# A hybrid encoder layer on one core: the gate of block 1 ahead of block 0's last denominators, one residual and its store near the end

## The chip, the cores and the metric

The kernel runs on one core of one Trainium2 chip. The metric is the time of one execution in device microseconds (us); lower is better. Five engines work side by side, each through its own queue in program order: TensorE (PE, matmuls), VectorE (DVE), ScalarE (ACT), GpSimd (POOL), and SyncE (SP), which issues all DMAs of this kernel. Engines wait for each other through semaphores.

## What is computed

The layer takes x (4096 tokens of 1024 numbers, float32), normalises it, projects it once to queries, keys, values, two gates and a pooling input, runs windowed attention and multi-scale pooling side by side, and adds the normalised output projection to x:

```
h = rmsnorm(x, pre_norm_g)
q, k, v, g_a, u_p, g_p = split(h @ w_in)
a = banded_attention(q, k, v, rel_bias, attn_sink) * silu(g_a)   # |i-j| <= 128
p = multiscale_pool(u_p, pool_w, pool_scale) * silu(g_p)
mixed = concat([a, p]) @ w_out
x = x + rmsnorm(mixed, post_norm_g)
```

There are 8 query heads of 64 and 2 key/value heads. Attention works in blocks of 128 queries, each against its own block of keys and the two beside it, with a sink logit in the denominator.

## The kernel before, in words

Matrix products run in float16, every float32 operand being split into a high and a low half and three of the four products of halves summed in PSUM.

The first half of the program forms the gates g_a and g_p and the pooling, and leaves their results in DRAM. The second half, which the change touches, goes through the tokens from the end to the start in units of 256 tokens (u = 15 down to 0), each of two blocks of 128 (block b = 2u and 2u + 1). Per unit it projects keys, values and queries, and then for each block:

- `scores(b, half)`: PE writes the logits of four heads (a half) to the PSUM tiles `s0` and `s1`.
- `logits(b, half, i)`: DVE adds the bias to a head's logits and finds the row extremum, from PSUM into the SBUF tile `p` (line 1295, a main instruction and a short one that reads `nm`). The first of the four issues a small POOL copy.
- `exps`: ACT takes the exponential and the row sum (line 1306); `denominators`: DVE scales the sums and takes reciprocals (lines 1313 and 1316).
- `probs` and `rests`: ACT writes the high half of the normalised probabilities (line 1328), DVE the low half (line 1336), both in `pn`; `turn`: a transposing DMA on SP puts them into `pt` (line 1345).
- `values(b, bank)`: PE multiplies `pt` with the values into two PSUM tiles, `o` and one named `p` in the bank `acc0`, `acc1` or `acc2` that the call names (line 1438; for block 0 the second tile is `s1`).
- `gate(b)`: DVE multiplies both tiles with the gate g_a into `at` (line 1462, two instructions). With that the two PSUM tiles are free.

The output projection of a unit is made from seven products in a Strassen-like scheme (`product`, line 1588, of inputs "11", "12", "22" and the sums "s1" to "s4"), and for unit 0 from eight plain ones (`last_product`, line 1560; its accumulators are named `z`, one of them lying in `s0`). `high` (ACT, line 1490) and `low` (POOL or DVE, line 1494) split an input of a product; `add` (DVE, line 1627) sums products into the output tile, `gain` (line 1622) multiplies it with post_norm_g, `square` (ACT) and `mean` (DVE line 1640 and POOL line 1645) give the factor `rs`, `residual(u, i, ...)` (DVE, line 1649) scales it and adds x, and `store` (SP, line 1655) writes it out. The residual of unit u with i = 1 is that of block 2u.

The accumulator of `last_product(1, "22", O22, 1, True)`, the first product for the right 512 columns of block 0, lies in `acc2`. The last earlier user of `acc2` is `values(1, 2)`. So this product can start only when `gate(1)` has read that tile. Likewise `last_product(0, "12", O21, 0, True)` writes `acc1` and needs the `add` that reads unit 1's product "s4" out of it.

The order of every engine's work is written out by hand: each step is entered with a number (`due(t, ...)`, or `at_(t, ...)` relative to the start `z` of the last stretch), all steps are sorted by that number, and each engine's instructions are issued in that order. The number is no time; it only sets the order. `ending(u, i, tm, tr)` enters a `mean` at `tm`, a `residual` at `tr` and its `store` at `tr + 1.3`. The change is in the last stretch, which holds the last part of unit 2, and units 1 and 0.

Of the kernel before, what the change touches and what calls it, by code (L numbers as in the profile page):

```python
# [134 lines left out]
def hybrid_layer(ctx: ExitStack, tc, io, out):  # L135
# [1107 lines left out]
    def due(t, fn, *args):  # L1243
        plan.append((t, len(plan), fn, args))
# [505 lines left out]
    def at_(t, fn, *args):  # L1750
        due(z + t, fn, *args)
# [11 lines left out]
    def cast(th, tw, u, name, f, eng):  # L1763
        at_(th, high, u, name, f)
        at_(tw, low, u, name, f, eng)

    def ending(u, i, tm, tr, split=False):
        at_(tm, mean, u, i)
        for n, cs in enumerate((LO, HI) if split else (slice(0, D),)):
            at_(tr + 0.7 * n, residual, u, i, cs)  # L1770
            at_(tr + 1.3 + 0.7 * n, store, u, i, cs)
# [187 lines left out]
    at_(12.3, square, 2, 0, 1)  # L1959
    at_(11.1, gain, 2, 1, LO, V)  # L1960
    at_(11.8, gain, 2, 1, HI, V)
    ending(2, 1, 10.9, 23.0)
    at_(38.7, gain, 2, 0, HI, V)
    ending(2, 0, 13.8, 39.4)

# [27 lines left out]

    cast(24.7, 26.1, 0, "22", a22, G)
    cast(34.35, 35.0, 0, "12", a12, G)
    at_(37.0, gate, 1)
    cast(37.6, 38.6, 0, "11", a11, V)
    at_(45.9, gate, 0)
    cast(46.7, 47.3, 0, "21", a21, V)
# [95 lines left out]
```

## Time and profile before

| what | value |
|---|---|
| median of 3 runs | 1182.24 us (1181.93 to 1183.64) |
| the profiled execution, whole | 1181.88 us |
| its span in the profile | 1179.9 us |
| PE busy | 1150.8 us, 98% of the span, 14304 matmuls |
| DVE busy | 932.0 us, 79% |
| ACT busy | 702.7 us, 60% |
| POOL busy | 310.2 us, 26% |

The span runs from the first to the last recorded instruction; the whole execution is 1.98 us longer. Times in the trace count from the start of the span. In the timeline, columns are start, duration, engine, line, operation, output and inputs, shape and count; brackets at the end give the idle time of the engine before the row and what ended it. Matmuls are pipelined, so a row's end overlaps the next row's start a little.

### The profile page before, as it was taken

To read this page: it belongs to the slowest core of one execution; us is meant where nothing else is said; L and a number is where in the kernel's file an instruction comes from. 1 tells how busy PE (TensorE), PEld (TensorE's weight loads), DVE (VectorE), ACT (ScalarE), POOL (GpSimd) and SP (SyncE) were. 2 spreads that over 40 slices of the span, in tenths; PEclk is the share of its full clock that TensorE was granted. 3 is DMA by queue.
4 is the path that set the end of the run, shared out by engine and by line. 5 is a ranking of instruction groups with operands and counts; after the bars stand their busy time and mean duration, and the time that the engine had idled before them with its cause. 6 is when DMAs were issued, how large, how long until landed. Compare 5 with 4: busy or idle time off the path is not lost. (4 is left out here: it accounts for less than half of the span.)

```text
span 1179.9 us, 33946 instructions
## 1 busy us (share of the span) xinstructions
PE 1150.8 (98%) x14304; PEld 883.7 (75%) x14304; DVE 932.0 (79%) x1865; ACT 702.7 (60%) x1459; POOL 310.2 (26%) x310
## 2 busy tenths in 40 slices
PE   5999999999999999999999999999999999999987
PEld 4998888888888888986677576666767667666643
DVE  6889997858788983568877877887787797788785
ACT  5875655545655542257676566667667666666761
POOL 0002111101101110201534433533443353254231
PEclk9999999999999999999999999999999999999998
DMA  8644487577757574299985777786687678686783
GB/s 314 217 111 166 161 270 261 178 239 229 239 188 236 158 188 159 67 275 245 222 198 141 189 193 149 188 197 184 137 188 205 140 196 184 176 169 154 190 205 107
DMA packets 292441, 224.65 MB, mean 190 GB/s; under 512 B 210704, under 2 KB 251920, under 8 KB 287680
## 3 DMA queue, kind: packets, MB, share of 16 engines
q1 hardware_dynamic: 292288, 222.48, 69.5%
q8 instruction: 112, 1.84, 0.6%
q14 instruction: 41, 0.34, 0.1%
HBM read 113.37 MB, written 60.33 MB: 147 GB/s over the span
## 5 line engine op out<-in xcount | busy, mean ns | idle before, releaser
L634 PEld LDWEIGHTS <-wq 128*128 128x128 f16 x4104 | 401.4, 98 | 52.8 <-issue 2.8
L634 PE MATMUL y<-xt,wq 128*128 128x256 f16 x1512 | 204.1, 273 | 0.9 <-ACT cc L742 0.9
L1306 ACT ACTIVATE p<-p,nm 128x385 f32<-128x385 f32 (+1 forms) x256 | 152.8, 599 | 37.1 <-POOL p L1289 20.4
L1227 PE MATMUL aq<-xb,xb 128*128 128x256 f16 x1024 | 173.4, 273 | 0.1
L1588 PE MATMUL ms<-wo,ys 128*128 128x512 f16 x720 | 162.7, 379 | 0.3 <-DVE mo L1627 0.3
L1336 DVE SCALAR_TENSOR_TENSOR pn<-p,rd,pn 128x384 f16<-128x384 f32 (+1 forms) x256 | 156.0, 660 | 6.4 <-ACT pn L1328 6.4
L1295 DVE CUSTOM_DVE_ANT_0 p<-s,nt,nsink 128x384 f32<-128x384 f32 (+1 forms) x256 | 155.9, 665 | 1.8 <-PE s L1272 1.7
L1227 PEld LDWEIGHTS <-xb 128*128 128x128 f16 x1280 | 125.2, 98 | 22.6 <-issue 6.3
L1227 PE MATMUL aq<-xb,xt 128*128 128x256 f16 x512 | 139.6, 273 | 0.0
L1328 ACT ACTIVATE pn<-p,rd 128x384 f16<-128x384 f32 (+1 forms) x256 | 134.5, 596 | 4.2 <-issue 1.1
L1588 PEld LDWEIGHTS <-ys 128*128 128x128 f16 x720 | 69.1, 98 | 81.6 <-issue 3.1
L304 POOL TENSOR_TENSOR yt<-yt,sg 128x512 f32<-128x512 f32 (+2 forms) x32 | 47.9, 1498 | 311.4 <-DVE yt L307 307.2
L1588 PE MATMUL m<-wo,y 128*128 128x512 f16 x540 | 121.8, 379 | 0.0
L1588 PEld LDWEIGHTS <-y 128*128 128x128 f16 x540 | 51.4, 98 | 63.0 <-issue 2.9
L1622 POOL TENSOR_TENSOR mo<-mo,gpost 128x512 f32<-128x512 f32 x39 | 63.8, 1635 | 94.6 <-ACT jkb L1611 93.4
L634 PE MATMUL plain<-xb,wq 128*128 128x256 f16 x576 | 68.8, 276 | 3.0 <-ACT xb L446 1.8
L1227 PEld LDWEIGHTS <-xt 128*128 128x128 f16 x640 | 62.6, 98 | 8.3
L634 PE MATMUL y<-xb,wq 128*128 128x256 f16 x504 | 68.8, 273 | 0.0
L634 PE MATMUL v<-xb,wq 128*128 128x256 f16 x504 | 68.6, 273 | 0.2 <-DVE cc L304 0.2
L634 PE MATMUL v<-xt,wq 128*128 128x256 f16 x504 | 68.6, 273 | 0.0
L634 PE MATMUL x<-xb,wq 128*128 128x256 f16 x504 | 68.2, 273 | 0.0
L1272 PE MATMUL s<-k_all,q 64*32 64x288 f16 (+7 forms) x3648 | 62.7, 266 | 2.1 <-DVE nm L1295 1.2
(212 smaller groups left out, 1911.6 us busy)
## 6 DMA issues: line engine op xcount, KB each, us to landing
nt<-in_xT SPq DMA_DIRECT2D x28, 512.0 KB, 5.1
x_scr<-xb SPq DMA_DIRECT2D x14, 1024.0 KB, 7.2
xb<-x_scr SPq DMA_DIRECT2D x14, 1024.0 KB, 7.1
xr<-in_x SPq DMA_DIRECT2D x28, 512.0 KB, 4.6
out<-xr SPq DMA_DIRECT2D x28, 512.0 KB, 2.6
xn<-in_x SPq DMA_DIRECT2D x27, 512.0 KB, 4.4
ga_scr<-cc SPq DMA_DIRECT2D x64, 128.0 KB, 2.4
raw<-in_w_out SPq DMA_DIRECT2D x16, 512.0 KB, 5.4
```

Of the source, the lines that this page charges most:

```text
L304: eng.tensor_tensor(out=out, in0=in0, in1=in1, op=op)
L634: nc.tensor.matmul(b[:, s], wq[:, slot[q, op], wv, s, k, :], x[:, xv, k, :], start=(first and k + s + wv + xv == 0), stop=(last and k == H ...
L1227: nc.tensor.matmul(acc, w[:, j, k, :], x[:, kh, v, kt, :], start=(n == 0), stop=(n == 3 * KT - 1),)
L1272: nc.tensor.matmul(s_ps[qs, gg, c0:c1], q_t[u, half][a, qi, jj, tl + 32 * hq : tl + 32 * hq + 32], k_all[a, ki, kc + c0 - s0 : kc + c1 - s ...
L1295: nc.vector.tensor_tensor_reduce(out=p_t[b, half][:, hh, :nk], in0=s_t[jj][:, gg, :nk], in1=bias[:, h, lo : lo + nk], scale=negc[:, h : h ...
L1306: nc.scalar.activation(p[:, hh, : nk + 1], p[:, hh, : nk + 1], AF.Exp, bias=nm_t[b, half][:, hh : hh + 1], scale=-1.0, accum_out=den_t[b, ...
L1328: nc.scalar.activation(prob_view(b, half)[:, 0, i], p_t[b, half][:, i, :nk], AF.Copy, scale=rd_t[b, half][:, i : i + 1],)
L1336: nc.vector.scalar_tensor_tensor(out=pn4[:, 1, i], in0=p_t[b, half][:, i, :nk], scalar=rd_t[b, half][:, i : i + 1], in1=pn4[:, 0, i], op0= ...
L1588: nc.tensor.matmul(z_t[u, tag], y[:, k, yi, :], wo[o][:, wi, k, :], start=(n == 0 and acc is None), stop=(n == 3 * HK - 1), skip_group_che ...
L1622: eng.tensor_tensor(out=mo, in0=mo, in1=gpost[:, cs], op=ALU.mult)
```

## The change

Two numbers in the list are changed: the residual of unit 2 with i = 1 (and its store), and the gate of block 1.

```diff
-    ending(2, 1, 10.9, 23.0)
+    ending(2, 1, 10.9, 38.2)
...
-    at_(37.0, gate, 1)
+    at_(33.9, gate, 1)
     cast(37.6, 38.6, 0, "11", a11, V)
```

No instruction is added or removed. On VectorE, at the end of the softmax of block 1, there stands before: the last low halves of block 1 (`pn_1_18718`), the residual (`xr_18224`), and then the logits of block 0's first half.

```order
L1336 SCALAR_TENSOR_TENSOR pn_1_18718<-p_1_18616,rd_1_18615,pn_1_18718 128x384 x2
L1627 TENSOR_TENSOR xb_68<-ms_1_18705,xb_68 128x512
L1336 SCALAR_TENSOR_TENSOR pn_1_18718<-p_1_18616,rd_1_18615,pn_1_18718 128x384 x2
L1649 SCALAR_TENSOR_TENSOR xr_18224<-mo_1_17912,rs_1_18459,xr_18224 128x1024
L1295 ISA p_0_18751,nm_0_18748<-s_5946,nt,nsink,negc 128x256
L1295 ISA nm_0_18748 128x1
```

With the change the logits follow the low halves directly (buffer numbers shift by a few):

```order
L1336 SCALAR_TENSOR_TENSOR pn_1_18718<-p_1_18616,rd_1_18615,pn_1_18718 128x384 x2
L1627 TENSOR_TENSOR xb_68<-ms_1_18705,xb_68 128x512
L1336 SCALAR_TENSOR_TENSOR pn_1_18718<-p_1_18616,rd_1_18615,pn_1_18718 128x384 x2
L1295 ISA p_0_18749,nm_0_18746<-s_5946,nt,nsink,negc 128x256
L1295 ISA nm_0_18746 128x1
```

The residual has left this place; every DVE row after it stands one place earlier.

Further on, still on VectorE, after the last of the logits of block 0's second half, there stand before: the denominators (`den_1`, `rd_1`), the low halves (`pn_1`), the `add` of unit 1's product "s4", the two instructions of block 1's gate (`at`), and the low half of input "11" (`xt_67<-at`).

```order
L1295 ISA nm_1_18858 128x1
L1313 TENSOR_SCALAR den_1_18859<-den_1_18859 128x4
L1316 RECIPROCAL rd_1_18860<-den_1_18859 128x4
L1336 SCALAR_TENSOR_TENSOR pn_1_18962<-p_1_18861,rd_1_18860,pn_1_18962 128x256 x4
L1627 TENSOR_TENSOR xb_68<-ms_1_18757,xb_68 128x512
L1462 SCALAR_TENSOR_TENSOR at_18988<-o_18867,gaf,gb_18400 128x4x64
L1462 SCALAR_TENSOR_TENSOR at_18988<-p_18866,gaf,gb_18400 128x4x64
L1494 TENSOR_TENSOR xt_67<-at_18988,xt_67 128x4x128
```

With the change:

```order
L1295 ISA nm_1_18856 128x1
L1462 SCALAR_TENSOR_TENSOR at_18944<-o_18865,gaf,gb_18400 128x4x64
L1462 SCALAR_TENSOR_TENSOR at_18944<-p_18864,gaf,gb_18400 128x4x64
L1313 TENSOR_SCALAR den_1_18857<-den_1_18857 128x4
L1316 RECIPROCAL rd_1_18858<-den_1_18857 128x4
L1336 SCALAR_TENSOR_TENSOR pn_1_18963<-p_1_18859,rd_1_18858,pn_1_18963 128x256 x4
L1627 TENSOR_TENSOR xb_68<-ms_1_18755,xb_68 128x512
L1649 SCALAR_TENSOR_TENSOR xr_18224<-mo_1_17912,rs_1_18459,xr_18224 128x1024
L1494 TENSOR_TENSOR xt_67<-at_18944,xt_67 128x4x128
```

The gate has moved ahead of the denominators, past seven instructions, and the residual now stands behind the `add`, before the low half of "11".

On SP, the store of that residual (`out<-xr_18224`) moves from behind block 1's last transposing DMA (`pt_1`, 24 tiles) to behind both of block 0's (`pt_0` and `pt_1`, 16 tiles each); the load of the pooling input (`yf`) and both transposes move up by one.

```order
 L1658 DMA wo_5956<-w_scr 128x4096
-L1345 DMA_TRANSPOSE pt_1_18742<-pn_1_18718 128x24x128
+L1345 DMA_TRANSPOSE pt_1_18741<-pn_1_18718 128x24x128
+L1517 DMA yf_0_18774<-yp_scr 128x512
+L1345 DMA_TRANSPOSE pt_0_18862<-pn_0_18844 128x16x128
+L1345 DMA_TRANSPOSE pt_1_18973<-pn_1_18963 128x16x128
 L1655 DMA out<-xr_18224 128x1024
-L1517 DMA yf_0_18776<-yp_scr 128x512
-L1345 DMA_TRANSPOSE pt_0_18864<-pn_0_18846 128x16x128
-L1345 DMA_TRANSPOSE pt_1_18972<-pn_1_18962 128x16x128
 L1655 DMA out<-xr_18226 128x1024
```

PE, ACT and POOL have the same instructions in the same order as before.

## The prediction

> **What bounds the kernel now.** PE is busy for 98% of the span (table above), so I ask first where it still waits in the second half of the program. The view of waits, for PE alone from 850 us to the end, has two rows:
>
> ```profile
> PE z L1560 <- DVE at L1462: 4.0, 1, 4.0
> PE s L1272 <- DVE nm L1295: 1.2, 2, 0.8
> ```
>
> Both name DVE, and both are places of the change: line 1462 is the gate, line 1295 the logits. The timeline of PE shows where they lie (in brackets, the wait):
>
> ```profile
> 1130.46 7.94 PE L1588 MATMUL ms<-wo,ys 128*128 128x512 f16 x36
> 1139.18 0.52 PE L1272 MATMUL s<-k_all,q 64*32 64x160 f16 x24 [0.78 <-DVE nm L1295]
> 1140.11 0.52 PE L1272 MATMUL s<-k_all,q 64*32 64x160 f16 x24 [0.41 <-DVE nm L1295]
> 1140.71 2.75 PE L1560 MATMUL z<-wo,xt 128*128 128x512 f16 x12
> ...
> 1145.32 2.76 PE L1588 MATMUL ms<-wo,ys 128*128 128x512 f16 x12
> 1152.06 7.04 PE L1560 MATMUL z<-wo,xt 128*128 128x512 f16 x24 [3.98 <-DVE at L1462]
> ```
>
> The first 24 of a 128x512 product after the long wait take 7.04 us. The chain that ended last says what the same count costs later, and that everything from here to the end hangs on it:
>
> ```profile
> 1151.22 0.80 DVE at L1462 x2
> ...
> 1152.06 7.04 PE z L1560 x24
> 1159.10 2.59 PE s L1560 x12
> ...
> 1163.27 2.70 PE z L1560 x12
> ...
> 1168.56 5.19 PE z L1560 x24
> ```
>
> From 1152 us on PE has no further wait, and 6.1 us of square, factor, residual and store follow its end at 1173.75. So the end moves with PE, and PE with DVE's order. The 7.04 against 5.19 us is explained by the clock in the table of windows (columns: window, length, busy time of PE, PEld, DVE, ACT, POOL, then granted clock):
>
> ```profile
> 1150.00:1152.00 2.00, 0.00 (x0) 0.00 (x0) 2.00 (x5) 0.00 (x0) 0.00 (x0) 1.00 0.05 9
> 1154.00:1155.50 1.50, 1.50 (x5) 0.55 (x4) 1.48 (x3) 0.00 (x0) 0.00 (x0) 0.50 0.27 51
> 1157.00:1159.00 2.00, 2.00 (x11) 0.94 (x10) 1.70 (x2) 0.00 (x0) 0.78 (x2) 1.00 0.21 86
> ```
>
> The clock is still full while PE idles, falls to 0.50 shortly after it has started again, and is back by 1157. The wait thus costs a second time, 7.04 - 5.19 = 1.85 us.
>
> **The change part by part.** Now what DVE does around it:
>
> ```profile
> 1136.03 2.17 DVE L1649 SCALAR_TENSOR_TENSOR xr<-mo,rs,xr 128x1024 f32<-128x1024 f32 x1
> 1138.12 0.53 DVE L1295 CUSTOM_DVE_ANT_0 p<-s,nt,nsink 128x256 f32<-128x256 f32 x1
> ...
> 1139.98 0.68 DVE L1627 TENSOR_TENSOR xb<-ms,xb 128x512 f32<-128x512 f32 x1
> ...
> 1141.49 0.69 DVE L1627 TENSOR_TENSOR xb<-ms,xb 128x512 f32<-128x512 f32 x1
> ...
> 1144.69 0.54 DVE L1295 CUSTOM_DVE_ANT_0 p<-s,nt,nsink 128x256 f32<-128x256 f32 x1
> ...
> 1147.44 0.17 DVE L1313 TENSOR_SCALAR den<-den 128x4 f32<-128x4 f32 x1 [0.81 <-ACT p L1306]
> ...
> 1150.54 0.68 DVE L1627 TENSOR_TENSOR xb<-ms,xb 128x512 f32<-128x512 f32 x1
> 1151.14 0.47 DVE L1462 SCALAR_TENSOR_TENSOR at<-o,gaf,gb 128x256 f32<-128x256 f32 x1
> ...
> 1152.69 0.69 DVE L1494 TENSOR_TENSOR xt<-at,xt 128x512 f16<-128x512 f32 x1 [0.68 <-ACT xt L1490]
> 1153.30 0.68 DVE L1622 TENSOR_TENSOR mo<-mo,gpost 128x512 f32<-128x512 f32 x1
> 1154.02 1.28 DVE L1649 SCALAR_TENSOR_TENSOR xr<-mo,rs,xr 128x1024 f32<-128x1024 f32 x1
> ...
> 1159.28 1.28 DVE L1649 SCALAR_TENSOR_TENSOR xb<-xb,rs,xb 128x1024 f32<-128x1024 f32 x1
> 1163.32 0.48 DVE L1462 SCALAR_TENSOR_TENSOR at<-o,gaf,gb 128x256 f32<-128x256 f32 x1 [2.75 <-PE o L1438]
> ...
> 1164.88 0.69 DVE L1494 TENSOR_TENSOR xt<-at,xt 128x512 f16<-128x512 f32 x1 [0.69 <-ACT xt L1490]
> ```
>
> *The residual leaves its place.* It stands directly ahead of block 0's first logits, which PE's next scores wait for. Without it the logits start at 1136.03, not 1138.12: 2.09 us earlier. Their PSUM tiles were written long before (the scores ahead of the row at 1130.46). The second scores could start when the 36 products end at about 1138.40 (1130.46 + 7.94); by then two of the logits have been read, and the other two by 1137.95 (1139.98, where the next row began, less 2.09). Both waits go: 0.78 + 0.41 = **1.19 us**. The `add` of the product that ends at 1138.40 moves from 1141.49 to 1139.40, still behind it. So the whole DVE row, and ACT's exponentials with it, move up by 2.09, and the logits of the second half run from 1142.60 to 1144.55.
>
> *The gate moves forward.* It needs `values(1)`, which ended where the row at 1145.32 begins; 1.19 earlier that is 1144.13. DVE arrives at 1144.55, so the gate does not wait and is over at 1144.55 + 0.88 (1151.14 to 1152.02, where the gate ends in the chain) = 1145.4, not 1152.02. PE ends product "s4" at about 1148.08 - 1.19 = 1146.9 (1148.08 is 1152.06 less the wait) and finds `acc2` free 1.5 us ago. The wait goes: **3.98 us**; and with no idle stretch, the slow clock: **1.85 us**.
>
> Behind the gate stand block 0's last denominators. They waited 0.81 us for ACT before, and the 0.88 us of the gate fill that gap, so they begin at about 1145.4, still 2.05 earlier than before. The `add` of "s4" begins at 1148.5 and ends at 1149.1. That is the next thing PE needs: the second 12 of the 24 products write `acc1`, from 1146.9 + 2.6 = 1149.5. Spare: 0.4 us, the thinnest place. The input of these products (ACT's and POOL's halves of "12") moves with the same 2 us.
>
> *The residual at its new place* runs from 1149.1. There it should take 1.28 us as at 1154.02, not 2.17. At its old place a POOL operation lay beside it that was long too, 2.13 us where the same operation takes 1.16:
>
> ```profile
> 1137.08 2.13 POOL L1494 TENSOR_TENSOR xt<-yf,xt 128x512 f16<-128x512 f32 x1
> ...
> 1148.00 1.16 POOL L1494 TENSOR_TENSOR xt<-yf,xt 128x512 f16<-128x512 f32 x1 [8.65 <-ACT xt L1490]
> ```
>
> The second row moves up to about 1145.9 and is over before the residual starts. [...]
>
> Behind the residual comes the low half of "11" at 1150.3. Before, it waited 0.68 us for ACT's high half, which had waited 2.43 us for the gate:
>
> ```profile
> 1152.04 0.62 ACT L1490 CAST xt<-at 128x512 f16<-128x512 f32 x1 [2.43 <-DVE at L1462]
> ```
>
> Now the gate is early, and ACT starts it when it is free, at 1152.04 - 2.43 - 2.05 = 1147.6: done two microseconds before DVE asks. DVE's block of gains and residuals therefore starts at 1150.9 instead of 1153.30 and ends at 1160.56 - 2.4 = 1158.2. PE has moved by more: 1.19 + 3.98 + 1.85 = 7.02. `values(0)` would end at 1163.27 - 7.02 = 1156.25, so `gate(0)`, which had 2.75 us of spare DVE time ahead of it, is now the one that waits, until 1158.2. This is **what is late next**. Its consumer is the last 24 products, at 1168.56 - 7.02 = 1161.54. From the gate to the end of its low half it took 1163.32 to 1165.57 (the rows of gate and low half, the latter 1164.88 + 0.69), 2.25 us; so it is ready at 1160.45, 1.1 us in time. Covered.
>
> *The store* moves behind block 0's two transposes. Before, they ran like this:
>
> ```profile
> L1345 SPq DMA_TRANSPOSE pt<-pn x2: 2062/2533/3004, 1144.8 to 1150.7; - x2
> DMA to landing us min/median/max: 5.4/5.4/5.4
> ```
>
> and block 1's transpose before them, and all 64 of the program, like this:
>
> ```profile
> L1345 SPq DMA_TRANSPOSE pt<-pn x1: 3945/3945/3945, 1136.1 to 1136.1; - x1
> DMA to landing us min/median/max: 5.5/5.5/5.5
> ...
> L1345 SPq DMA_TRANSPOSE pt<-pn x64: 2062/3822/6321, 512.0 to 1150.7; - x64
> DMA to landing us min/median/max: 5.4/6.5/9.1
> ```
>
> The last one now starts at about 1148.6 and lands at 1154.0. `values(0)` starts at 1149.5 + 2.6 + 2.6 = 1154.7 and needs it half a microsecond later: 1.2 us spare. The store can begin when the residual is done, about 1150.4, while the transpose is on its way. What that does to the transpose no row shows. From below: nothing (5.4 us again). From above: the longest landing in the whole trace, 9.1 us, that is 1157.7 and a wait of 2.5 us. I take nothing, since the transpose's data has been moving for a while when the store starts; and the store itself is done long before the last ones.
>
> *Sum.* 1.19 + 3.98 + 1.85 = 7.02 us off the profiled execution's 1181.88: 1174.9. That execution lay 0.36 us under the median of 1182.24, so the median should be near **1175.1**, a gain of 0.6%.
>
> [...]
>
> **The rivals.**
>
> *A new wait for the last transpose (8%).* For it: the 512 KB store now starts into its landing, and landings up to 9.1 us exist. Against: 5.4 here, and 1.2 us spare. At 9.1 PE waits 2.5 us: 1175.1 + 2.5 = 1177.6.
>
> *DVE becomes the bound at gate(0) or at `acc1` (12%).* The spare is 1.1 and 0.4 us. If two of the residuals were stretched from 1.28 to 2.17, `gate(0)` would be 1.8 late and 0.7 would reach PE; if the `add` came 1 us later, 0.6. Both: 1176.4.
>
> *The clock falls anyway (5%).* The low clock appeared 1 us after PE had resumed, so the wait as its cause is inferred. If it stays, 1.85 are not saved: 1177.0.
>
> *The gate blocks DVE (2%), the case on the other side.* Ahead of the denominators, a gate that waits holds up denominators, low halves, the last transpose and the `add`. It waits if `values(1)` is late, and that hangs on block 1's transpose, issued at 1136.13 and needed at about 1142.1, 6.0 us later. A landing later than 6.0 + 7.0 = 13 us, or about 11 us with the clock lost again, makes the kernel slower than before; at 16 us it would be 10 + 1.85 above my forecast, 1187. It landed in 5.5 us before, and the longest is 9.1; nothing new lies ahead of it on SP.
>
> *The change does not do what it says (3%).* PE might need something else at 1146.9 that was hidden by the gate: then part of the 3.98 stays, and with a rest under 2 us the time is 1177 to 1179. All other inputs of that product date from before 1140.
>
> **How the numbers follow.** My forecast as computed has 70%. The first three rivals and the last stay below 1178 in most of their cases, so the upper end is 1178.0. The lower end is 1174.0: the forecast from the fastest run shown (1181.93 - 7.02 = 1174.9), less 0.9 more if the low halves or DVE's tail gain as well, for which I have no row. Differences within 0.2% (2.4 us) can hardly be told from no change. Faster by more than that is all that ends below 1179.8: 95%; within it 3%; slower 2%.
>
> **What would show it.** Right: PE's waits from 850 us lose both rows; the granted clock is 1.00 from 1130 us to the end of PE's work; the 24 products after "s4" take about 5.2 us; the moved residual takes about 1.3; `gate(0)` no longer waits for PE but follows DVE's last residual. Wrong: a wait of PE for `pt`, for an `add`, or for the low half of "21" with a length above a few tenths, or a clock below 1.00 before 1165.

## The result and the profile after

| | before | after |
|---|---|---|
| median, us | 1182.47 (1181.45 to 1183.64, 6 runs) | 1175.03 (1174.83 to 1175.62, 6 runs) |
| the profiled execution, us | 1181.88 | 1174.91 |
| its span, us | 1179.9 | 1172.8 |

The ratio of the times is 0.9938, 95% interval 0.9925 to 0.9951: 0.6% faster, 1175.03 where 1175.1 was forecast. The runs also scatter less, over 0.8 us instead of 2.2. One of the 15 runs of the kernel before that were made beside experiments 5 to 8 took 1999.18 us at an average granted clock of 0.56; medians and ratios below leave it out.

The view of PE's waits from 850 us to the end of the changed kernel has one row where there were two:

```profile
PE z L1560 <- DVE xb L1627: 0.2, 1, 0.2
```

Neither the gate (L1462) nor the logits (L1295) are waited for; what is left is a wait of 0.15 us (0.2 in the view) for the `add` of product "s4", in the place that the prediction called the thinnest. PE's timeline of the changed kernel:

```profile
1130.50 7.94 PE L1588 MATMUL ms<-wo,ys 128*128 128x512 f16 x36
1138.38 0.85 PE L1272 MATMUL s<-k_all,q 64*32 64x160 f16 x48
1139.16 2.77 PE L1560 MATMUL z<-wo,xt 128*128 128x512 f16 x12
1143.77 2.76 PE L1588 MATMUL ms<-wo,ys 128*128 128x512 f16 x12
1146.38 2.75 PE L1560 MATMUL z<-wo,xt 128*128 128x512 f16 x12
1149.28 2.75 PE L1560 MATMUL z<-wo,xt 128*128 128x512 f16 x12 [0.15 <-DVE xb L1627]
...
1161.32 5.34 PE L1560 MATMUL z<-wo,xt 128*128 128x512 f16 x24
```

The first products of unit 0's right columns follow "s4" at once, at 1146.38. The two groups of 12 that were one row of 7.04 us are 5.65 us now, wait included. The table of windows of the changed kernel has the granted clock (third number from the end) at 1.00 right through to the end of PE's work:

```profile
1146.00:1152.00 6.00, 5.85 (x28) 2.58 (x27) 5.51 (x9) 2.85 (x7) 1.16 (x1) 1.00 0.61 119
1152.00:1158.00 6.00, 6.00 (x70) 3.27 (x68) 5.48 (x8) 0.00 (x0) 2.21 (x2) 1.00 0.65 251
1158.00:1166.70 8.70, 8.67 (x41) 3.72 (x38) 5.26 (x10) 2.58 (x7) 0.54 (x1) 1.00 0.28 109
```

And DVE's timeline of the changed kernel, with the rows that answer to those shown of before:

```profile
1136.12 0.53 DVE L1295 CUSTOM_DVE_ANT_0 p<-s,nt,nsink 128x256 f32<-128x256 f32 x1
...
1144.55 0.48 DVE L1462 SCALAR_TENSOR_TENSOR at<-o,gaf,gb 128x256 f32<-128x256 f32 x1
1144.95 0.48 DVE L1462 SCALAR_TENSOR_TENSOR at<-p,gaf,gb 128x256 f32<-128x256 f32 x1
1145.45 0.17 DVE L1313 TENSOR_SCALAR den<-den 128x4 f32<-128x4 f32 x1
...
1148.55 0.68 DVE L1627 TENSOR_TENSOR xb<-ms,xb 128x512 f32<-128x512 f32 x1
1149.15 1.27 DVE L1649 SCALAR_TENSOR_TENSOR xr<-mo,rs,xr 128x1024 f32<-128x1024 f32 x1
...
1156.92 1.28 DVE L1649 SCALAR_TENSOR_TENSOR xb<-xb,rs,xb 128x1024 f32<-128x1024 f32 x1
1158.12 0.48 DVE L1462 SCALAR_TENSOR_TENSOR at<-o,gaf,gb 128x256 f32<-128x256 f32 x1
...
1159.68 0.69 DVE L1494 TENSOR_TENSOR xt<-at,xt 128x512 f16<-128x512 f32 x1 [0.69 <-ACT xt L1490]
```

and POOL's operation that lay beside the residual at its old place:

```profile
1137.17 1.15 POOL L1494 TENSOR_TENSOR xt<-yf,xt 128x512 f16<-128x512 f32 x1
```

The gate of block 1 starts at 1144.55 with no wait and fills the time (0.81 us) in which DVE used to wait for ACT. The moved residual takes 1.27 us instead of 2.17, and POOL's operation 1.15 instead of 2.13. `gate(0)` (1158.12) has no wait in front of it any more: it follows DVE's last residual, as forecast, and its low half is ready at 1160.37, 0.95 us before PE asks for it at 1161.32.

### The profile page after: what moved, and what is told of

It is laid out like the page before. It is cut to its first block, busy times and chain, and to the rows that moved or that the text cites. A ratio compares the mean times of both kernels' runs of the same rounds, so it can differ in the third digit from the quotient of the medians.

```text
span 1172.8 us, 33945 instructions
## 1 busy us (share of the span) xinstructions
PE 1149.0 (98%) x14304; PEld 883.4 (75%) x14304; DVE 930.8 (79%) x1865; ACT 702.6 (60%) x1459; POOL 309.3 (26%) x310
## 4 chain that ended last, share of the span: by engine, by line
PE 50%; DVE 1%; ACT 0%; issue 0%; DVEq 0%; POOLq 0%; ACTq 0%
PE ms L1588 13%; PE aq L1227 12%; PE m L1588 9%; PE s L1272 4%; PE kv L1373 3%; PE o L1438 3%; PE kv L1227 3%; PE p L1438 2%; PE z L1560 1%; PE s L1560 0%; DVE pn L1336 0%; DVE mo L1627 0%; DVE p L1295 0%; ACT pn L1328 0%; DVE xt L1649 0%
## 5 line engine op out<-in xcount | busy, mean ns | idle before, releaser
L1295 DVE CUSTOM_DVE_ANT_0 p<-s,nt,nsink 128x384 f32<-128x384 f32 (+1 forms) x256 | 155.9, 665 | 1.8 <-PE s L1272 1.7
```

What stands on the lines that cost most here:

```text
L1295: nc.vector.tensor_tensor_reduce(out=p_t[b, half][:, hh, :nk], in0=s_t[jj][:, gg, :nk], in1=bias[:, h, lo : lo + nk], scale=negc[:, h : h ...
```

## The experiments

Eight kernels were run in two groups of four, each group beside the kernel before (median 1182.05 in the first group, 1182.26 in the second). The changed kernel was run at another time, beside a median of 1182.47; a ratio compares a kernel with the runs of the kernel before made beside it. "Average clock" is the granted clock averaged over a whole execution; the 3.41 us at a clock of 0.50 that three traces show (last section) lower it by 0.0014, by arithmetic (3.41 x 0.50 / 1180).

### One part alone

Experiment 1 has only the residual and its store at the new place.

```diff
-    at_(33.9, gate, 1)
+    at_(37.0, gate, 1)
```

> Only the residual and its store are at the late place; block 1's gate is back behind the low halves and the add. Theory (each part worth what its wait costs): the two waits of PE for the logits (1.19 us) stay gone; the gate runs from 1149.15 to 1150.03, so PE waits about 3.5 us for it after product s4, from 1146.5 to 1150.05. [...] Rival (the gain comes from the residual, the gate's place hardly matters): about 1175 to 1176.

Measured: 1178.95 us (1177.30 to 1180.15, 7 runs), ratio 0.9971 [0.9960, 0.9982]. The gate's place matters: with it back, more than half of the gain is gone. PE's timeline of this kernel:

```profile
1137.70 0.85 PE L1272 MATMUL s<-k_all,q 64*32 64x160 f16 x48
...
1149.42 6.75 PE L1560 MATMUL z<-wo,xt 128*128 128x512 f16 x24 [3.56 <-DVE at L1462]
```

The scores run in one piece, so the two short waits belong to the residual alone. The wait for the gate is 3.56 us, as expected from the rows, and the clock was lost in the profiled execution (6.75 us for 24 products). I had estimated 1178.6 us (1175.0 + 3.5) with a full clock and about 1180.4 with the clock lost as after the 3.98 us, without a choice between the two. The seven runs lie on both sides of 1178.6 and reach up to 1180.15.

Experiment 2 has only the gate at the new place.

```diff
-    ending(2, 1, 10.9, 38.2)
+    ending(2, 1, 10.9, 23.0)
```

> Only the gate is at the early place; the residual is back ahead of block 0's logits. Theory: the two short waits for the logits are back (1.19 us), the long wait and the low clock are gone; the add of s4 ends about 2.1 us later than in the changed kernel while PE asks for it only 1.2 us later, so the wait for it grows from 0.15 to about 0.8 us. Time 1175.0 + 1.2 + 0.6 = 1176.8; the moved residual takes 2.17 us again. Rival (residual gives the gain): 1181 to 1182.

Measured: 1176.78 us (1176.51 to 1177.45), ratio 0.9957 [0.9944, 0.9969]: the expected number. PE's waits of this kernel from 850 us on:

```profile
PE s L1272 <- DVE nm L1295: 1.3, 2, 0.8
PE z L1560 <- DVE xb L1627: 0.6, 1, 0.6
```

The two short waits are back, the long one is not, and the wait for the `add` has grown from 0.15 to 0.62. So the gate's move is worth the larger part, and the residual's move adds 1.75 us to it by the medians (1176.78 - 1175.03; 2.2 by the ratios): its own two waits (1.3) and the head start that DVE needs for the `add` (0.62 - 0.15). Alone, the residual gains 3.10 us and the gate 5.27 against 1182.05, 8.4 together, more than the 7.4 of both at once: in part because the early residual also shortens the wait for the gate (3.56 instead of 3.98 us), which the early gate takes away in any case. The residual in DVE's timeline of this kernel, and the operation beside it in POOL's:

```profile
1135.72 2.18 DVE L1649 SCALAR_TENSOR_TENSOR xr<-mo,rs,xr 128x1024 f32<-128x1024 f32 x1
```

```profile
1136.78 2.14 POOL L1494 TENSOR_TENSOR xt<-yf,xt 128x512 f16<-128x512 f32 x1
```

At the old place both are long again.

### The gate's place, step by step

Three kernels move only the gate, with the residual as in the changed kernel. In experiment 3 it stands between the low halves and the `add`.

```diff
-    at_(33.9, gate, 1)
+    at_(36.4, gate, 1)
```

> As the changed kernel, but the gate stands between the low halves and the add. [...]

Measured: 1179.60 us (1177.67 to 1180.98, 10 runs), ratio 0.9977 [0.9968, 0.9987]. The first row is PE's timeline, the second the table of windows, with the granted clock third from the end:

```profile
1149.32 7.03 PE L1560 MATMUL z<-wo,xt 128*128 128x512 f16 x24 [2.95 <-DVE at L1462]
```

```profile
1150.00:1152.00 2.00, 2.00 (x7) 0.73 (x6) 2.00 (x3) 0.62 (x2) 0.00 (x0) 0.53 1.15 212
```

Before the run I had estimated a wait of about 2.9 us for the gate, none for the `add`, and 1177.9 us (1175.0 + 3.0 - 0.1). The wait is 2.95 us, but the clock falls all the same (0.53 on average in this window, 0.50 in most of it), and the 24 products take as long (7.03 us) as after 3.98 us (7.04). That this wait keeps the clock was my estimate alone, and it fell; 1179.7, the estimate with the clock lost as after 3.98 us (1177.9 + 1.85), is close to the median. The two fastest runs, 1177.67 and 1178.13, lie where a full clock would put them, but their average clocks, 0.998 and 0.997, do not confirm it.

In experiment 4 it stands between the first and the second of the logits.

```diff
-    at_(33.9, gate, 1)
+    at_(32.15, gate, 1)
```

> As the changed kernel, but the gate stands still earlier, between the first and the second of the logits of block 0's second half. Theory (a gate that waits blocks DVE): DVE reaches it at 1143.2 and waits until values(1) end at about 1143.9; logits, denominators, low halves and add come 1.6 us later; PE waits for the add about 1.7 us instead of 0.15; the last transpose lands 1.6 us later, just in time. Time 1175.0 + 1.6 = 1176.6, clock full. Rival (earlier is better or makes no difference, because PE is free to go on): 1175.0 or less.

Measured: 1175.83 us (1175.57 to 1176.68), ratio 0.9950 [0.9937, 0.9962]. The median lies 0.8 us above that of the changed kernel, by the ratios the difference is 1.4, but the two intervals overlap. What the early gate does is plain in DVE's and PE's timelines:

```profile
1143.39 0.48 DVE L1462 SCALAR_TENSOR_TENSOR at<-o,gaf,gb 128x256 f32<-128x256 f32 x1 [0.67 <-issue]
```

```profile
1150.22 2.75 PE L1560 MATMUL z<-wo,xt 128*128 128x512 f16 x12 [1.63 <-DVE xb L1627]
```

DVE stands still 0.67 us at the gate. The view names no engine for this, but PE's row of product "s4", which follows `values(1)`, begins at 1143.23, just before the gate's 1143.39. Everything behind the gate is late, and PE waits 1.63 us for the `add` instead of 0.15. The wait is the expected one. The median stayed 0.8 us below the expected 1176.6, which had been set on the changed kernel's 1175.0; the kernel before ran 0.42 us faster beside this experiment than beside the changed kernel, and by the ratios 1.4 of the expected 1.6 us are there. Single executions differ more: the row of 36 products, ahead of the first changed instruction, begins anywhere from 1129.83 (experiment 1) to 1130.50 (the changed kernel) in the traces of before, of the changed kernel and of experiments 1 to 4.

In experiment 6 it stands between the second and the third of the low halves.

```diff
-    at_(33.9, gate, 1)
+    at_(35.5, gate, 1)
```

> As the changed kernel, but the gate stands between the second and the third of block 0's last low halves. Theory: PE waits about 2.0 us for the gate after product s4, nothing for the add: 1175.0 + 2.0 - 0.15 = 1176.9 with a full clock. [...] Rival (the loss follows any wait over about 1 us): 1178.6 in all.

Measured: 1177.82 us (1176.78 to 1178.80, 5 runs), ratio 0.9962 [0.9950, 0.9975]. PE's timeline of the profiled execution, the fastest of the five:

```profile
1148.66 5.34 PE L1560 MATMUL z<-wo,xt 128*128 128x512 f16 x24 [2.16 <-DVE at L1462]
```

Here the wait of 2.16 us left the clock alone (5.34 us; average clock 1.000), and the time is the 1176.9 that was expected. Of the other four, three have an average clock of 0.997 and times of 1177.82 to 1178.80; the fourth is between (0.998, 1177.23). By these averages, and by times near 1178.6 (1176.9 and a lost clock) in two of them, this wait cost the clock in at least three of five runs, though none of the three was profiled. I had expected few or none, an estimate, and it was wrong.

### Is it the idle PE that takes the clock down?

Experiment 5 is the kernel before, with 14 extra products in the long wait. They are not part of the computation and nobody reads them.

```diff
+    def filler(n):
+        y = y_t[0, "22"]
+        for i in range(n):
+            nc.tensor.matmul(
+                s_t[0][:, 1], y[:, 0, 0, :], wo[O22][:, 0, 0, :],
+                start=True, stop=True, skip_group_check=True,
+            )
...
     at_(34.2, product, 1, "s4", O22, 1, True)
+    at_(36.7, filler, 14)
     at_(36.8, last_product, 1, "22", O22, 1, True)
```

> The kernel before, with 14 extra products of 128x512 on PE between product s4 and the first product that waits for block 1's gate; they go to a free half of s0 and nobody reads them. Theory (the idle PE takes the clock down): they fill about 3.0 of the 3.98 us of the wait, under 1 us of it stays, the granted clock stays 1.00, the 24 products behind take 5.2 us instead of 7.0, and the time falls by about 1.8 us, to 1180.2 against 1182.05 before, although PE does more work; the scatter of the runs shrinks to about 1 us. Rival (the clock falls for another reason): 1182.

Measured: 1180.12 us (1179.38 to 1181.52, 11 runs) against 1182.26, ratio 0.9982 [0.9973, 0.9991]. PE's timeline of this kernel, and its table of windows around the 24 products:

```profile
1148.95 3.19 PE L1668 MATMUL s<-wo,xt 128*128 128x512 f16 x14
1153.11 5.35 PE L1560 MATMUL z<-wo,xt 128*128 128x512 f16 x24 [0.98 <-DVE at L1462]
```

```profile
1150.00:1156.00 6.00, 5.02 (x24) 2.13 (x23) 5.28 (x10) 1.90 (x5) 0.20 (x1) 1.00 0.58 112
```

More work on PE made the kernel faster: the clock stays at 1.00, and the 24 products behind the wait take 5.35 us instead of 7.04, although the gate stands at its old place. With 0.98 us of idle PE instead of 3.98 the fall does not come, so here the low clock goes with the idle time. The scatter did not shrink to 1 us as I had expected; it is 2.1.

### The residual's place, and the last wait

Experiment 7 puts the residual directly behind the gate.

```diff
-    ending(2, 1, 10.9, 38.2)
+    ending(2, 1, 10.9, 33.95)
```

> As the changed kernel, but the moved residual stands directly behind the gate, ahead of the denominators. Theory: denominators, low halves, add and the last transpose come 1.2 us later, PE waits about 1.3 us for the add instead of 0.15: 1176.2, clock full; if the residual and POOL's low half of input 12 stretch each other, 0.9 more. Rival (any place behind the first logits is as good, as DVE has time): 1175.0.

Measured: 1176.40 us (1175.78 to 1177.26), ratio 0.9951 [0.9938, 0.9963]. DVE's timeline, and POOL's:

```profile
1145.28 1.28 DVE L1649 SCALAR_TENSOR_TENSOR xr<-mo,rs,xr 128x1024 f32<-128x1024 f32 x1
1146.47 1.13 DVE L1313 TENSOR_SCALAR den<-den 128x4 f32<-128x4 f32 x1
```

```profile
1145.94 1.63 POOL L1494 TENSOR_TENSOR xt<-yf,xt 128x512 f16<-128x512 f32 x1 [7.54 <-ACT xt L1490]
```

The residual, followed within 1.2 us by the denominators, delays them by that much, and then the first of them, usually 0.17 us, takes 1.13 beside POOL's operation and ends with it. PE waits 1.74 us for the `add`. So DVE has time for the residual, but not at every place: of the three places tried, only the one behind the `add` that PE waits for cost nothing.

Experiment 8 is the changed kernel with the `add` of "s4" ahead of the last low half.

```diff
-    at_(36.5, add, 1, (0, HI), (0, HI), 1)
+    at_(36.0, add, 1, (0, HI), (0, HI), 1)
```

> The changed kernel with the add of product s4 one place earlier, ahead of the last of block 0's low halves. Theory: the add ends about 0.5 us sooner, the last wait of PE in this stretch (0.15 us) goes, the transpose starts 0.6 us later and is still in time: 1174.9, 0.15 below the changed kernel, which only the trace can show. Rival (the transpose becomes late): a wait for pt, 1175.5.

Measured: 1174.94 us (1174.10 to 1175.11, 5 runs), ratio 0.9936 [0.9923, 0.9948]. The view of PE's waits from 850 us on is empty, and the 24 products are one row again in PE's timeline:

```profile
1146.98 5.34 PE L1560 MATMUL z<-wo,xt 128*128 128x512 f16 x24
```

The last wait is gone. By the times, 0.09 us under the changed kernel, the two cannot be told apart. The transpose was not late.

## Why the prediction was right, step by step

- *The end moves with PE, and PE with DVE's order.* Right. PE's work ended at 1173.75 and ends at 1166.68 (the chain's last row, 1161.49 + 5.19), 7.07 us earlier; the span is 7.1 us shorter. (Two small slips in the working change nothing: 1182.24 - 7.02 is 1175.2, not 1175.1, and 1139.98 - 2.09 is 1137.89, not 1137.95.)
- *The residual, 1.19 us.* Right in mechanism, too small in size: "s4" starts at 1143.77 instead of 1145.32, 1.55 us. The waits in the view leave out what PE loses in stopping and starting: two rows of scores took 0.52 us each where one of the same 48 products takes 0.85, and rows that follow each other overlap a little in the timeline (by 0.15 us at 1146.38), which they do not across a wait.
- *The gate, 3.98 us.* From the start of "s4" to the start of the products that waited it was 6.74 us (1152.06 - 1145.32) and is 2.61: 4.13 us, for the same reason.
- *The clock, 1.85 us.* Gone, but worth less here: the 24 products spread over 6.88 us from their start to that of the next group (1152.06 to 1158.94) and over 5.49 now (1146.38 to 1151.87), 1.39 us. These 5.49 us contain the new wait of 0.15 and its restart; and against the timeline's own row of 24 (5.34) the loss was 1.70, where I had set the chain's shortened 5.19. The prediction had the fall shortly after PE starts again, as in the kernel before (1153.21, PE from 1152.06); in experiment 1 it came while PE was still idle (1148.88, PE from 1149.42). That the sum fits so closely is luck: the two waits were set 0.51 us too small together, the clock 0.46 too large, and 1.55 + 4.13 + 1.39 = 7.07 against 7.02.
- *The denominators lose nothing behind the gate.* Right: they begin at 1145.45, forecast 1145.4.
- *`acc1`, 0.4 us spare.* Off by 0.55: PE would have come at about 1149.0 (1146.38 + 2.61), half a microsecond earlier than computed, while the `add` ended at 1149.23 (1148.55 + 0.68) instead of 1149.1; PE waits 0.15.
- *The residual at its new place, 1.28 us.* Right, 1.27, and POOL's operation at the old place went from 2.13 to 1.15. Experiments 2 and 7 agree: apart both are short (1.27 and 1.15 in the changed kernel); overlapping, POOL's is long (2.14 and 1.63), and so is the residual in experiment 2 (2.18) and the operation behind it in experiment 7 (1.13 instead of 0.17).
- *`gate(0)` follows DVE, 1.1 us in time.* Right, 0.95.
- *The transpose with the store behind it.* It landed in 4.3 us, less than the 5.4 that the prediction took as its lower bound, so the open cost was none. In every experiment the store moved together with its residual, so no run shows the store's place alone; PE never waited for `pt` in any of the eight.
- *The rivals.* That the clock falls for another reason is refuted by experiment 5, where it stayed at 1.00 with 0.98 us of the wait left. That a gate that waits blocks DVE is shown to exist by experiment 4 (0.67 us), at a small price. What length of wait costs the clock was my estimate before experiments 1, 3 and 6, and no run shows a limit: 2.95 us took the clock in experiment 3, and 2.16 us left it alone in the profiled execution of experiment 6. No term of the sum rested on it, since the longest wait that was left is 0.15 us.

## What to carry to other kernels

Where one engine is busy all the time, look for its few waits near the end and ask which instruction of another engine, in a queue of its own, releases them; moving that one instruction ahead of work that nobody waits for so soon cost nothing here. Each term could be summed from the rows to about half a microsecond. Work without a consumer, like a residual and its store, stood best here behind the last instruction that the busy engine needs (a wait of 0.15 us), not in the first gap behind the gate (1.74 us, experiment 7); and a releasing instruction moved too early held up its queue (0.67 us, experiment 4). An idle PE cost a second time here, up to 1.70 us for the clock, after waits of 2.16 to 3.98 us and not in every run; no run shows that cost after 1.74 us or less.

## What the runs showed of the hardware that was not expected

Whether the clock is lost does not follow from the length of PE's wait alone, and it differs from run to run. Sorted by PE's longest wait in this stretch of the profiled execution, with the average clock of the runs:

| kernel | wait, us | 0.997 or below | 0.998 | 0.999 or above |
|---|---|---|---|---|
| before (beside experiments 1 to 4) | 3.98 | 15 | 0 | 1 |
| before (beside experiments 5 to 8) | same kernel | 13 | 1 | 0 |
| experiment 1 | 3.56 | 3 | 4 | 0 |
| experiment 3 | 2.95 | 9 | 1 | 0 |
| experiment 6 | 2.16 | 3 | 1 | 1 |
| experiment 7 | 1.74 | 0 | 0 | 5 |
| experiment 4 | 1.63 | 0 | 1 | 4 |
| experiment 5 | 0.98 | 0 | 5 | 6 |
| experiment 2 | 0.85 | 0 | 0 | 5 |
| changed kernel | 0.15 | 0 | 0 | 6 |
| experiment 8 | none | 0 | 1 | 4 |

In the traces of the kernel before and of the changed kernel the clock also falls to 0.50 after PE's last product, at 1177.10 and 1170.39, 2.8 and 2.4 us before the end of the span. By arithmetic that alone lowers the average by 0.0012 and 0.0010; a loss in this stretch lowers it by another 0.0014. So I take 0.997 as a clock lost before PE's end and 0.999 as one that was not, an estimate from these lengths, and 0.998 can be either: the profiled execution of experiment 1 lost the clock here at 0.998, and those of experiments 4, 5 and 8 have 0.998 with a full clock here. Eleven runs, ten of them of the kernel before, have 0.996; the two places take 0.0026 from the average in the profiled execution of the kernel before, which is less, and no profile shows where those runs had the rest. Where the average is 1.000, with 3.98 us in one run of the kernel before (1180.87 us) and with 2.16 us in one of experiment 6 (1176.78 us), the time is the lowest of its kernel, though a run of the kernel before with 0.997 took only 1180.88.

The table of windows in steps of 0.25 us has the ends of the low clock: the kernel before (two rows), experiment 1 (two) and experiment 3 (two).

```profile
1153.00:1153.25 0.25, 0.25 (x3) 0.13 (x2) 0.25 (x1) 0.25 (x2) 0.00 (x0) 0.92 1.19 219
1156.50:1156.75 0.25, 0.25 (x2) 0.15 (x1) 0.25 (x1) 0.00 (x0) 0.25 (x1) 0.75 1.07 442
```

```profile
1148.75:1149.00 0.25, 0.00 (x0) 0.00 (x0) 0.25 (x2) 0.00 (x0) 0.00 (x0) 0.76 0.00 0
1152.25:1152.50 0.25, 0.25 (x2) 0.10 (x1) 0.25 (x1) 0.00 (x0) 0.00 (x0) 0.91 0.95 393
```

```profile
1150.00:1150.25 0.25, 0.25 (x3) 0.08 (x2) 0.25 (x1) 0.25 (x1) 0.00 (x0) 0.74 1.12 216
1153.50:1153.75 0.25, 0.25 (x2) 0.10 (x1) 0.25 (x3) 0.00 (x0) 0.00 (x0) 0.93 0.02 0
```

Interpolated, the clock was at 0.50 from 1153.21 to 1156.62, from 1148.88 to 1152.30 and from 1150.12 to 1153.53: 3.41 us each time, whatever the wait (3.98, 3.56 or 2.95), beginning 3.0 to 5.1 us after PE had stopped. The loss is half of the low time in which PE works: 1.70 us (7.04 - 5.34) and 1.69 (7.03 - 5.34) where all 3.41 us fell on work, 1.41 (6.75 - 5.34) in experiment 1, where the fall came 0.54 us before PE started again.

What sets the moment of a fall, and which waits bring one, no run shows. By the averages a wait of 3.98 us cost the clock in 28 of 30 runs, one of 2.95 us in 9 of 10 and one of 2.16 us in 3 of 5; after 1.74 us or less no run shows a loss, and the 0.78 and 0.41 us of the kernel before left the clock at 1.00 (1130 to 1152 us).

The last transpose landed in 4.3 us in the six traces in which the moved store stands behind it on SP (the changed kernel, experiments 1, 3, 4, 6 and 8), and in 5.4 and 5.3 us in the kernel before and in experiment 5, in which the store stands ahead of it. So in these eight traces the difference goes with the store's place; by what mechanism is open.
